# TensorE's program order relisted by due dates, and a rearranged opening with filler products, in a two-layer trunk on eight cores

## Chip, cores, metric

One Trainium2 chip, 8 cores: each computes one sample of the batch. The metric is device time in microseconds, of the slowest core; lower is better. In some executions, whatever the kernel, one die or both run at a lower granted clock (the share of its full clock that TensorE is given) and the time is longer, by up to 18% here. A run is called slow, and left out of times and ratios, when one die's cores took over 1% longer than the other's at a lower clock, or the time is over 1.5% above the kernel's fastest.

## The reference

```python
D_MODEL, BATCH, SEQ, DEPTH, D_FF = 1024, 8, 2048, 2, 2816

def modulate(x, g, mod):                      # mod: shift, scale, gate
    shift, scale, gate = jnp.split(mod, 3, axis=-1)
    h = rmsnorm(x, g) * (1.0 + scale[:, None, :]) + shift[:, None, :]
    return h, gate[:, None, :]

def swiglu(h, w_in, w_out):
    g, u = jnp.split(h @ w_in, 2, axis=-1)
    return (jax.nn.silu(g) * u) @ w_out

def reference(x, c, norm_g, w_mod, b_mod, w_ffn_in, w_ffn_out, ...):
    c_act = jax.nn.silu(c)
    for l in range(DEPTH):
        mod = c_act @ w_mod[l] + b_mod[l]
        mod_f1, mod_mx, mod_f2 = jnp.split(mod, 3, axis=-1)
        h, gate = modulate(x, norm_g[l, 0], mod_f1)
        x = x + 0.5 * gate * swiglu(h, w_ffn_in[l, 0], w_ffn_out[l, 0])
        # ... the mixer (gating and short convolution, or causal pooling) ...
        # ... a second half-step SwiGLU ...
    return rmsnorm(x, final_g)
```

What matters here: no product of layer 0 can start before its shift and scale rows are there (16 rows of the modulation matrix, 512 KB each: 8 MB), and before half of x (two tiles of 2 MB) has been loaded and its statistics taken.

## The kernel before

The program is written as a list of operations, each with what it reads and writes and a modelled cost. A first pass places them in listing order. A second, `relist`, simulates the machine again and lets the engines named in `free` take, of the operations that are ready in the model, the one with the earliest due date; the other engines keep the first pass's order. Each engine then runs its list strictly in order. TensorE was not free: its order was the listing's.

```python
    def relist(self, free=("dve", "act")):
        # ... cost[] and due[] of every operation: due = its start in the first listing
        #     (plus 8 us if it isn't TensorE's), pulled ahead by what depends on it ...
        fixed = {e: [] for e in self.ENGS if e not in free}
        for o in sorted(ops, key=lambda o: (o.start, o.idx)):
            if o.eng in fixed:
                fixed[o.eng].append(o.idx)
        # ... events in order of model time t; for each idle engine e:
                elif e in ready:                       # a free engine
                    if not ready[e]:
                        continue
                    _, x = heapq.heappop(ready[e])     # ready, earliest due
                else:                                  # a fixed engine waits for its next one
                    if at[e] >= len(fixed[e]) or not isready[fixed[e][at[e]]]:
                        continue
```

The opening, where the 16 rows become shift and scale of the 8 chunks of 128 channels: a row's dot product with the conditioning vector is either 8 one-column TensorE matmuls in f32 (16 instructions in the profile) or one VectorE pass. A weight slot is a buffer for one weight piece; its "gate" is the chunk after whose row the slot's load is asked for.

```python
    order0 = [0, 4, 1, 5, 2, 6, 3, 7]                     # order in which chunks are made
    on_pe = (0, 2, 4, 6, 8, 10, 12, 14, 15)               # rows (by position) dotted on TensorE
    rows0 = [q for c in order0 for q in (c, 8 + c)]
    # ... row0_dma(n): one 512 KB load;  row0(k): both rows of chunk order0[k] ...
    for k in range(early // 2):
        row0(k)
    stats0(0)                                             # squares of x, summed by a product of ones
    # ...
    for k in range(ready0, NC):
        row0(k)
        # ... apply_chunk: normalise, scale, shift -> H; h_sums: sums of chunks for the fast product ...
    for s, k in zip(range(NSLOT), (3, 5, 6, 7, 7, 7)):    # "gates" of the six weight slots:
        load_next(s, [("MOD", 0, order0[k])])             # slot s is asked for after chunk order0[k]'s row
    # ...
                if k == 0 and g == 0:
                    run_segs(segs[:X_AT])                 # X_AT = 60
                    late_x()                              # second half of x: two loads of 2 MB
                    bg_add(stats_gen([2, 3]))
                    run_segs(segs[X_AT:-3])
    # ...
    Sd.relist()
```

Of the kernel before, what the change touches and what calls it, by code (L numbers as in the profile page):

```python
# [15 lines left out]
NC = 8  # L16
# [4 lines left out]
EPS = 1e-6  # L21
NSLOT = 6
STAGE = True
X_AT = 60


def keeps(sub, g, part, n):
# [434 lines left out]
def I(name, *a, **k):  # L462
    return lambda E: getattr(E, name)(*a, **k)  # L463
# [4 lines left out]
def build_nc():  # L468
# [28 lines left out]
    NSQ = 4  # L497
    SQ = sb("SQ", [128, NSQ, TT], BF16)
    CB = sb("CB", [128, D], F32)
    CT = sb("CT", [128, 8], F32)  # L500
# [5 lines left out]
    ONES = sb("ONES", [128, 128], BF16)  # L506
# [10 lines left out]
    PS = [nc.alloc_psum_tensor("ps%d" % b, [128, TT], F32) for b in range(8)]  # L517

    Sd = Sched()
# [12 lines left out]
    def c_pe(n):  # L532
        return n / 2400.0 + 0.0026

    def mm(out, lhsT, rhs, start, stop, reads, writes, n=TT):
        return add("pe", I("matmul", out, lhsT, rhs, start=start, stop=stop, skip_group_check=True), reads=reads, writes=writes,
                   cost=c_pe(n))
# [4 lines left out]
    def act(out, in_, func, reads, writes, n=TT, src="ps", **kw):  # L542
        op = add("act", I("activation", out=out, in_=in_, func=func, **kw), reads=reads, writes=writes, cost=c_act(n, src))
        if func in (AF.Silu, AF.Gelu_apprx_tanh):
            op.gate = set(last_root[0])
            table_ops.add(op.idx)
        return op

    def tt_(out, in0, in1, op, reads, writes, n=TT, half=False):
        return add("dve", I("tensor_tensor", out=out, in0=in0, in1=in1, op=op), reads=reads, writes=writes, cost=c_dve(n, half))  # L550

    def stt(out, in0, scalar, in1, op0, op1, reads, writes, n=TT, **kw):
        return add("dve", I("scalar_tensor_tensor", out=out, in0=in0, scalar=scalar, in1=in1, op0=op0, op1=op1, **kw),
                   reads=reads, writes=writes, cost=0.05 + c_dve(n))
# [30 lines left out]
    def Xv(c, t):  # L585
        return X[:, t, c, :]

    def Xk(c, t):
        return ("X", c, t)
# [225 lines left out]
    def bg_add(g):  # L815
        bg.append(g)
        if len(bg) == 1:
            bg_state[0] = 0.0
# [73 lines left out]
    def ones_mm(z, t, of=NC // 2):  # L892
        st = stat_state.setdefault(t, {"n": 0, "b": 6 + t % 2, "of": of})
        b = st["b"]
        mm(PS[b][:], ONES[:], SQ[:, z, :], st["n"] == 0, st["n"] == of - 1, [("SQ", z), "ONES"], [("ps", b)])
        st["n"] += 1
# [34 lines left out]
    def apply_chunk(l, s, p, c, tt, place, dest=None):  # L931
        t = 2 * p + tt
        o = (l * 3 + s) * 8
        sh = l * 72 + s * 24
        tm = tmp_rot.next()
        tt_(TP[:, tm, 0:TT], Xv(c, t), RS[:, t % 2, :], ALU.mult, [Xk(c, t), ("RS", t % 2)], [("TP", tm)])
        ap, key = dest if dest is not None else (place.ap(c, tt), place.key(c, tt))
        act(ap, TP[:, tm, 0:TT], AF.Identity, [("TP", tm)] + fin["k", l, s, c], [key], src="sb",
            scale=AS[:, o + c:o + c + 1], bias=MODT[:, sh + c:sh + c + 1])

    def h_sums(c0, w=2):

        def v(q):
            return H[:, (q * 4 + c0) * TT:(q * 4 + c0 + w) * TT]

        def k(q):
            return [("H", q * 4 + c0 + i) for i in range(w)]

        tt_(v(4), v(1), v(0), ALU.subtract, k(1) + k(0), k(4), n=w * TT, half=True)
        tt_(v(1), v(3), v(1), ALU.subtract, k(3) + k(1), k(1), n=w * TT, half=True)  # L950
        tt_(v(5), v(3), v(4), ALU.subtract, k(3) + k(4), k(5), n=w * TT, half=True)
        tt_(v(6), v(2), v(5), ALU.subtract, k(2) + k(5), k(6), n=w * TT, half=True)
# [547 lines left out]
    add("dve", I("memset", SQ[:, 0, :], 0.0), writes=[("SQ", 0)], cost=0.3)  # L1500
    for b in ALLB:
        mm(PS[b][:], ONES[:], SQ[:, 0, :], True, True, [("SQ", 0), "ONES"], [("ps", b)])
    order0 = [0, 4, 1, 5, 2, 6, 3, 7]
    on_pe = (0, 2, 4, 6, 8, 10, 12, 14, 15)
    early = 6
    mid = 1
    rows0 = [q for c in order0 for q in (c, 8 + c)]
# [4 lines left out]
    def row0_dma(n):  # L1512
        kind, w = places[n % npl]
        if kind == "W":
            ap, keys, dk = WM[:, w, :], [("WM", w)], ("WM", w)
        else:
            ap, keys, dk = Af32[:, w * 1024:(w + 1) * 1024], [("A", 4 * w + x) for x in range(4)], ("AM", w)
        src = wmod0_d[rows0[n]] if n in on_pe else wmod_d[rows0[n]]
        add("sp", I("dma_start", out=ap, in_=src), writes=keys, cost=0.06, dma=dk, nbytes=128 * 4096)
        stage0[n] = (ap, keys)  # L1520
# [3 lines left out]
    def row0(k):  # L1524

        c = order0[k]
        for n, q in ((2 * k, c), (2 * k + 1, 8 + c)):
            ap, keys = stage0[n]
            M = MODT[:, q:q + 1]
            shift = n % 2 == 0  # L1530
            fk = ("MOD", 0, c) if shift else ("ASc", c)
            if n in on_pe:
                b = banks0.next()
                for kc in range(NC):
                    add("pe", I("matmul", PS[b][:, 0:1], ap[:, kc * 128:(kc + 1) * 128], CT[:, kc:kc + 1], start=kc == 0,
                                stop=kc == NC - 1, skip_group_check=True), reads=keys + ["CT"], writes=[("ps", b)], cost=0.43)
                src, sk = PS[b][:, 0:1], [("ps", b)]
            else:
                stt(ap, ap, 1.0, CB[:], ALU.mult, ALU.mult, keys + ["CB"], [("MOD", 0, q)], n=1024, accum_out=M)
                for kk in keys:  # L1540
                    Sd.readers.setdefault(kk, []).append(len(Sd.ops) - 1)
                src, sk = M, [("MOD", 0, q)]
            if n + npl < 16:
                row0_dma(n + npl)
            if shift:
                tt_(M, src, SM[:, SM_BMOD + c:SM_BMOD + c + 1], ALU.add, sk + ["SM"], [fk], n=1)
            else:
                stt(AS[:, c:c + 1], src, SB1[:, c:c + 1], SM[:, SM_G + c:SM_G + c + 1], ALU.add, ALU.mult,
                    sk + ["SB1", "SM"], [fk], n=1)
        fin["k", 0, 0, c] = [("ASc", c), ("MOD", 0, c)]  # L1550
# [3 lines left out]
    for t in range(2):  # L1554
        add("sp", I("dma_start", out=X[:, t, :, :], in_=xT[t].rearrange("p (c k) -> p c k", k=TT)),
            writes=[Xk(c, t) for c in range(NC)], cost=0.06, dma=("X", t), nbytes=128 * 16384)
    for n in range(early, npl):
        row0_dma(n)
    def stats0(t):
        for c in range(NC):  # L1560
            z = sq_rot.next()
            act(SQ[:, z, :], Xv(c, t), AF.Square, [Xk(c, t)], [("SQ", z)], src="sb")
            ones_mm(z, t, NC)
        rstd([t], True, load=(1.3, 0.0) if t == 0 else (0.0, 0.0))

    for k in range(early // 2):
        row0(k)
    stats0(0)
    if mid:
        row0(early // 2)  # L1570
    stats0(1)
    tmp_rot.items = list(range(NTP))
    ready0 = early // 2 + mid
    for k in range(ready0):
        apply_chunk(0, 0, 0, order0[k], 0, HH)
    for k in range(ready0, NC):
        row0(k)
        if k == ready0:
            for j in range(ready0):
                apply_chunk(0, 0, 0, order0[j], 1, HH)  # L1580
                if j % 2 == 1:
                    h_sums(j // 2, 1)
        apply_chunk(0, 0, 0, order0[k], 0, HH)
        apply_chunk(0, 0, 0, order0[k], 1, HH)
        if k % 2 == 1:
            h_sums(k // 2, 1)
    tmp_rot.items = [6, 7]
    for q in range(16):
        done_rows.add(q)
    for b in (0, 1):  # L1590
        mm(PS[b][:], ONES[:], SQ[:, 0, :], True, True, [("SQ", 0), "ONES"], [("ps", b)])
    fin["n", 0, 0] = True
    for s, k in zip(range(NSLOT), (3, 5, 6, 7, 7, 7)):
        load_next(s, [("MOD", 0, order0[k])])
    for lm in range(2):
        for sm in range(3):
# [16 lines left out]
    def late_x():  # L1613
        for t in range(2, 4):
            add("sp", I("dma_start", out=X[:, t, :, :], in_=xT[t].rearrange("p (c k) -> p c k", k=TT)), reads=[("A", ablk(6, 0))],
                writes=[Xk(c, t) for c in range(NC)], cost=0.06, dma=("X", t), nbytes=128 * 16384)

    def run_segs(segs, side=iter(())):

        for n, f in enumerate(segs):  # L1620
            f()
            next(side, None)
            if n == 1:
                while carry:
                    carry.pop(0)()
            pump()
# [12 lines left out]
    for k, ph in enumerate(PHASES):  # L1639
# [4 lines left out]
        if sub[0] == "F":  # L1644
            l, i = sub[1], sub[2]
            s = 2 * i
            for g in range(len(GROUPS)):
# [15 lines left out]
                if k == 0 and g == 0:  # L1663
                    run_segs(segs[:X_AT])
                    late_x()
                    bg_add(stats_gen([2, 3]))
                    run_segs(segs[X_AT:-3])
                else:
# [14 lines left out]
                if pm is not None:  # L1683
                    if pm == 0:
                        add("dve", I("memset", STAT[:, 0, 15:16], 0.0), reads=[("MOD", 0, q) for q in range(144)],
                            writes=["PMFREE", "CB"] + [("WM", x) for x in range(NWM)] + [("ST", x) for x in range(4)], cost=0.05)
# [34 lines left out]
        marks.append((sub, p, t_begin, Sd.tl["pe"].tail()))  # L1721

    add("sp", None, reads=[("OUT", t, c) for t in range(4) for c in (1, 3, 5, 7)], cost=0.01)
    Sd.relist()
    with nc.Block() as block:
        Sd.emit(nc, block)
    nc._sched = Sd
# [33 lines left out]
```

## Time and profile before

| | kernel before |
|---|---|
| time, median of 3 fast runs | 1972.81 us (1972.31 to 1972.99) |
| spans of cores 0 and 1 | 1938.9, 1943.3 us |
| spans of cores 2 to 7 | 1961.1 to 1967.0 us |
| TensorE busy, slowest core | 1920.7 us, 98% of the span |
| first real product (all cores) | 58.2 to 60.1 us |
| TensorE idle from 100 to 165 us | 4.1 to 9.4 us |
| TensorE idle after 165 us | 10.5 to 13.1 us |

The clock row of the page gives the granted clock of TensorE in tenths, in 40 slices of 49 us (9 is 90% or more):

```profile
PEclk9887899999999999999999999999999999999998
```

Slices 2 to 5 (49 to 246 us) are the only dip before the last slice: there lies the throttled stretch that the prediction begins with. "Trip" stands below for such a stretch at a clock of 0.81.

### The profile page before, as it was taken

How to read it: one execution, taken by the hardware profiler on the slowest of the kernel's cores; microseconds unless marked ns; L12 is line 12 of the kernel's file. 1: busy time of each engine (PE TensorE's matmuls, PEld its weight loads, DVE VectorE, ACT ScalarE, POOL GpSimd, SP SyncE). 2: the span in 40 equal slices, each digit the busy share in tenths (PEclk: the TensorE clock that was granted, in tenths of full speed). 3: DMA queues.
4: the chain of work that ended last, by engine and by line, in shares of the span. 5: the costliest groups of instructions: out<-in, count | busy, mean ns of one | idle time of the engine just before them, and what ended most of it. 6: DMA issues, size and time to landing. Idle time of an engine off the chain costs nothing.

```text
span 1967.0 us, 25441 instructions; the slowest of 8 cores (1938.9 to 1967.0 us)
## 1 busy us (share of the span) xinstructions
PE 1920.7 (98%) x8750; PEld 874.8 (44%) x8750; DVE 1695.3 (86%) x3246; ACT 1032.8 (53%) x1738; POOL 172.2 (9%) x330
## 2 busy tenths in 40 slices
PE   6999999999999999999999999999999999999997
PEld 4533444444444444444444444444444444444443
DVE  3867899999798999999988888898998889888865
ACT  4443555455564655465455545564456555574343
POOL 0000000000202000000000000000000000000000
PEclk9887899999999999999999999999999999999998
DMA  9875668786777777776755554555454444445752
GB/s 283 164 186 121 135 130 171 172 171 138 158 161 173 162 152 172 157 154 135 169 105 86 86 86 85 87 97 86 76 86 70 84 84 86 75 75 86 173 87 95
DMA packets 66653, 248.72 MB, mean 126 GB/s; under 512 B 7520, under 2 KB 7648, under 8 KB 66016
## 3 DMA queue, kind: packets, MB, share of 16 engines
q0 software_dynamic: 42192, 153.64, 47.5%
q1 hardware_dynamic: 24336, 93.45, 14.4%
q8 instruction: 74, 1.21, 0.2%
q14 instruction: 51, 0.42, 0.1%
HBM read 392.29 MB, written 8.39 MB: 204 GB/s over the span
## 4 chain that ended last, share of the span: by engine, by line
PE 91%; DMA 4%; DVE 3%; ACT 1%; SPq 0%; issue 0%; DVEq 0%; POOLq 0%
PE ps L463 91%; DMA ACTB<-wmod 2%; DMA SLOTS<-wout 2%; DVE ACTB L463 1%; DVE SLOTS L463 1%; DVE X L463 0%; DVE WMOD L463 0%; SPq L463 0%; ACT PMH L463 0%; DVE TP L463 0%; ACT ps L463 0%; DVE ps L463 0%; ACT TP L463 0%; ACT L463 0%; ACT ACTB L463 0%
## 5 line engine op out<-in xcount | busy, mean ns | idle before, releaser
L463 PE MATMUL ps<-H,SLOTS 128*128 128x512 f16 x5440 | 1215.7, 383 | 6.6 <-ACT ps L463 2.2
L463 PEld LDWEIGHTS ps<-H,SLOTS 128*128 128x128 f16 x5440 | 534.9, 99 | 668.8 <-issue 83.7
L463 ACT ACTIVATE ps<-ps 128x512 f32<-128x512 f32 x684 | 398.0, 582 | 584.8 <-PE ps L463 548.6
L463 PE MATMUL ps<-ACTB,SLOTS 128*128 128x512 f16 x2780 | 622.5, 383 | 1.4 <-DVE TP L463 0.8
L463 PEld LDWEIGHTS ps<-ACTB,SLOTS 128*128 128x128 f16 x2780 | 273.7, 99 | 337.5 <-issue 30.6
L463 DVE TENSOR_TENSOR SLOTS<-SLOTS 128x512 f16<-128x512 f16 x996 | 395.2, 418 | 17.1 <-DMA SLOTS<-wout 8.0
L463 DVE SCALAR_TENSOR_TENSOR X<-ps,GH,X 128x512 f32<-128x512 f32 x424 | 308.3, 746 | 44.6 <-PE ps L463 37.6
L463 ACT ACTIVATE TP<-ps 128x512 f32<-128x512 f32 x400 | 238.0, 595 | 130.8 <-PE ps L463 130.5
L463 DVE TENSOR_TENSOR ACTB<-TP,ps 128x512 f16<-128x512 f32 x368 | 249.3, 684 | 46.4 <-PE ps L463 27.8
L463 ACT ACTIVATE SQ<-X 128x512 bf16<-128x512 f32 x224 | 131.4, 621 | 113.1 <-DVE X L463 57.9
L463 POOL DMA_DIRECT2D SLOTS<-win x176 | 93.1, 530 | 1046.0 <-PE ps L463 974.0
L463 DVE TENSOR_TENSOR TP<-ps,TP 128x512 f32<-128x512 f32 x176 | 121.2, 688 | 65.2 <-ACT ps L463 63.4
L463 DVE SCALAR_TENSOR_TENSOR WMOD<-WMOD,CB 128x1024 f32<-128x1024 f32 x129 | 156.8, 1218 | 2.8 <-DMA WMOD<-wmod 2.6
L463 DVE TENSOR_TENSOR TP<-X,RS 128x512 f32<-128x512 f32 x192 | 129.7, 686 | 12.5 <-ACT ACTB L463 8.5
L463 DVE TENSOR_TENSOR ps<-ps,TP 128x512 f32<-128x512 f32 x176 | 122.4, 696 | 15.2 <-PE ps L463 14.0
L463 DVE TENSOR_TENSOR ACTB<-ACTB 128x1024 f16<-128x1024 f16 (+1 forms) x188 | 104.6, 566 | 1.5
L463 POOL DMA_DIRECT2D SLOTS<-wout x88 | 46.5, 528 | 521.4 <-PE ps L463 521.4
L463 ACT ACTIVATE H<-TP,MODT,AS 128x512 f16<-128x512 f32 x81 | 62.7, 805 | 20.0 <-DVE TP L463 11.9
L463 PE MATMUL ps<-SQ,ONES 128*128 128x512 bf16 x130 | 44.7, 432 | 15.0 <-DVE SQ L463 6.7
L463 ACT ACTIVATE PMH<-TP,MODT,AS 128x512 f16<-128x512 f32 x60 | 47.6, 806 | 18.1 <-DVE TP L463 18.1
L463 ACT ACTIVATE ACTB<-TP,MODT,AS 128x512 f16<-128x512 f32 x51 | 40.8, 806 | 15.4 <-PE ps L463 12.5
L463 DVE TENSOR_TENSOR SQ<-SQ 128x1024 bf16<-128x1024 bf16 (+1 forms) x56 | 36.3, 649 | 12.2 <-ACT SQ L463 11.8
(74 smaller groups left out, 562.0 us busy)
## 6 DMA issues: line engine op xcount, KB each, us to landing
SLOTS<-win POOLq DMA_DIRECT2D x176, 512.0 KB, 6.0
WMOD<-wmod SPq DMA_DIRECT2D x131, 512.0 KB, 5.8
SLOTS<-wout POOLq DMA_DIRECT2D x88, 512.0 KB, 5.4
SLOTS<-wab POOLq DMA_DIRECT2D x28, 512.0 KB, 8.7
X<-xT SPq DMA_DIRECT2D x4, 2048.0 KB, 20.8
outT<-X SPq DMA_DIRECT2D x16, 512.0 KB, 3.7
ACTB<-wmod SPq DMA_DIRECT2D x13, 512.0 KB, 25.1
CB<-cb SPq DMA_DIRECT2D x1, 512.0 KB, 5.5
```

The source lines that it names most:

```text
L463: return lambda E: getattr(E, name)(*a, **k)
```

## The change

Intent: let TensorE step around products whose data is late (the second listing now orders TensorE too); start real products sooner (natural chunk order, so that the first group of chunks is complete early; only four rows dotted on TensorE; the first weight slots asked for sooner); and keep TensorE warm, that is at full clock, until then with 36 filler products of data that is already there. The late half of x, with its statistics, is also asked for five segments earlier in the listing (`X_AT`).

```diff
-X_AT = 60
+X_AT = 55
+WARM = 36
+SLG = (2, 3, 4, 6, 7, 7)
 ...
-    order0 = [0, 4, 1, 5, 2, 6, 3, 7]
-    on_pe = (0, 2, 4, 6, 8, 10, 12, 14, 15)
+    order0 = list(range(NC))
+    on_pe = (10, 12, 14, 15)
 ...                                   (modelled cost of a dot's matmul)
-                                ... writes=[("ps", b)], cost=0.43)
+                                ... writes=[("ps", b)], cost=0.25)
 ...
     stats0(1)
+    for n in range(WARM):
+        op = mm(PS[5][:], ONES[:], SQ[:, n % NSQ, :], True, True, [("SQ", n % NSQ), "ONES"], [("ps", 5)])
+        op.after = 28.0 + n * 0.6
+        op.start, op.end = op.after, op.after + op.issue
 ...
                 apply_chunk(0, 0, 0, order0[j], 1, HH)
-                if j % 2 == 1:
-                    h_sums(j // 2, 1)
 ...
-        if k % 2 == 1:
-            h_sums(k // 2, 1)
+        h_sums(k - 4, 1)
 ...
-    for s, k in zip(range(NSLOT), (3, 5, 6, 7, 7, 7)):
+    for s, k in zip(range(NSLOT), SLG):
 ...
-    Sd.relist()
+    Sd.relist(("dve", "act", "pe"))
```

More of the change, by code (lines that the diff above doesn't have):

```diff
@@ L1535, in row0 @@
                     add("pe", I("matmul", PS[b][:, 0:1], ap[:, kc * 128:(kc + 1) * 128], CT[:, kc:kc + 1], start=kc == 0,
-                                stop=kc == NC - 1, skip_group_check=True), reads=keys + ["CT"], writes=[("ps", b)], cost=0.43)
+                                stop=kc == NC - 1, skip_group_check=True), reads=keys + ["CT"], writes=[("ps", b)], cost=0.25)
                 src, sk = PS[b][:, 0:1], [("ps", b)]
```

## The prediction

> **What bounds the kernel now.** I read the page, then the cores, TensorE by stretch on a slow and a fast core, the first 75 us instruction by instruction, and what TensorE waits for.
>
> ```profile
> span 1967.0 us, 25441 instructions; the slowest of 8 cores (1938.9 to 1967.0 us)
> PE 1920.7 (98%) x8750; PEld 874.8 (44%) x8750; DVE 1695.3 (86%) x3246; ACT 1032.8 (53%) x1738; POOL 172.2 (9%) x330
> ```
>
> TensorE is full. Of the 46 us in which it is not, most lie in the opening. Its count of products is fixed by the algorithm, so time can come only from idle stretches, from products that run at a low clock, and from the opening. The stretches of the slowest core (3), then of core 0, with the granted clock third from the end:
>
> ```profile
> core 3: us, PE busy (x) PEld busy (x) DVE busy (x) ACT busy (x) POOL busy (x), PEclk, DMA share, GB/s
> 50.00:60.00 10.00, 9.60 (x45) 8.99 (x45) 9.21 (x26) 4.70 (x7) 2.12 (x4) 1.00 0.96 177
> ...
> 60.00:230.00 170.00, 163.61 (x619) 66.99 (x618) 129.46 (x249) 77.02 (x128) 11.09 (x21) 0.81 0.69 152
> ```
> ```profile
> 60.00:230.00 170.00, 162.27 (x732) 71.90 (x732) 149.38 (x295) 88.93 (x148) 13.26 (x25) 0.97 0.79 175
> ```
>
> Between 60 and 230 us core 3 gets through 619 products at a clock of 0.81, core 0 through 732 at 0.97. At full clock a product is 0.208 us (48 in 10 us on core 0), so the 113 missing ones are 24 us of the 28 us by which their spans differ. Cores 2 to 7 all have this: 0.81 from some 69 to 229 us, some 160 us, then full clock to the end. Cores 0 and 1 never have it. Busy time hides it.
>
> The opening is a chain of loads of modulation rows (8 MB in 16 rows) and of x, at the full rate of the DMA engines, and then of TensorE's dot products with the last rows:
>
> ```profile
> 48.38 3.55 PE L463 MATMUL ps<-CT,ACTB 128*128 128x1 f32 x16 [2.10 <-DMA ACTB<-wmod]
> 51.79 3.55 PE L463 MATMUL ps<-CT,WMOD 128*128 128x1 f32 x16
> 55.20 3.55 PE L463 MATMUL ps<-CT,ACTB 128*128 128x1 f32 x16
> 59.16 1.01 PE L463 MATMUL ps<-SQ,ONES 128*128 128x512 bf16 x2 [0.40 <-DVE AS L463]
> 59.96 10.46 PE L463 MATMUL ps<-H,SLOTS 128*128 128x512 f16 x42
> ```
> ```profile
> 59.54 0.15 PEld L463 LDWEIGHTS ps<-H,SLOTS 128*128 128x128 f16 x1 [0.28 <-issue]
> 59.96 0.15 PEld L463 LDWEIGHTS ps<-H,SLOTS 128*128 128x128 f16 x1 [0.28 <-issue]
> 60.39 0.15 PEld L463 LDWEIGHTS ps<-H,SLOTS 128*128 128x128 f16 x1 [0.28 <-issue]
> ```
>
> The first real product starts at 59.5 us, and weight loads 0.42 us apart show that TensorE is at half clock then, whatever the "1.00" of the stretch says (core 3's clock record begins only at 61.8 us). The waits after 100 us:
>
> ```profile
> PE ps L463 <- DVE SQ L463: 6.7, 4, 2.5
> PE ps L463 <- DVE CB L463: 3.3, 3, 1.8
> PE ps L463 <- DVE TP L463: 2.7, 2, 1.9
> PE ps L463 <- ACT ps L463: 2.2, 5, 0.7
> ```
>
> Gaps over 0.3 us after 100 us sum to 17.0: 6.3 in 129 to 153 us (late x tiles, second-half statistics), where the clock also falls to 0.5 for 6.8 us, and 10.8 in some fifteen places up to 1956.
>
> [...] a weight piece of 512 KB (1 MB in HBM) issued beside the row loads took 11 us (37.1 to 48.2), alone some 6.
>
> **The change, part by part.**
>
> *Fewer row dots on TensorE (9 to 4).* Five rows go to VectorE at 1.23 + 0.08 = 1.31 us each. Three of these land before 18 us, when VectorE is idle: free. Two come after 33 us: 2.6 us on top of the 23.3 us that VectorE is busy in 30 to 60 us. It fits, narrowly. TensorE is rid of 5 x 3.5 = 17.7 us, mostly spent waiting for loads anyhow.
>
> *Natural order.* A unit's first and fifth products (8 matmuls) need only chunks 0 to 3. Before, chunk 3 came seventh of eight; now it comes fourth, its rows landing near 36 us. So the two groups of units 0 and 1 (16 matmuls; the six PSUM banks let in no more) can run before chunk 7 is done.
>
> *Earlier weight slots.* Slot 0 is asked for at about 18 us rather than 37, slots 1 and 2 at 37 and 41 rather than 49 and 53. No byte is saved; they push back the rows. By the last row's landing (52.2) 1.5 MB of slots had moved; now some 2.7 MB, so at 0.33 MB/us that row lands 3.6 us later, near 55.8.
>
> *Fillers.* 36 products of ones with resident squares, from the end of the squares (near 36 us) on: 36 x 0.43 = 15 us cold, 8 warm, in time that is free. They warm the clock, so that the last dot takes some 2 us (the diff's new cost is 8 x 0.25) rather than 3.5.
>
> Sum of the opening. Before, the first product that needs chunk 7 came after 8 others: 59.96 + 8 x 0.43 = 63.4. Now: last row 55.8, dot 2.0, scale 0.3, normalised chunk 0.7 + 0.8 = 59.6, and 0.6 for VectorE's fuller queue, 60.2. That is 3.2 earlier, with 8 more products done (1.7): **5 us, between 0 and 9.**
>
> *TensorE relisted.* The second listing takes TensorE's operations as they get ready in its model, by due date. Products that wait in the model step aside; waits that the model does not foresee stay. From 129 to 153 us, 6.3 idle and 6.8 x (0.81 - 0.5) = 2.1 of clock: VectorE stood 5.05 us for an output weight piece slowed by the x tiles, which no TensorE order speeds up. I take 2.5 of 8.4. Of the 10.8 later on, a third: 3.5. An order fit to a model makes new waits: minus 2. **Net 4 us.**
>
> *The late x statistics* begin five segments earlier in the listing; the transfer still waits for the same activation block. Counted with the above.
>
> *The limiter.* If it trips on the dense f16 stream as now, its window moves with that stream and nothing changes. If the fillers trip it (25%), the window opens near 45 instead of 69 us and 24 x 0.19 = 4.5 us are saved; if a gentler start leaves every pair of cores untripped (7%), some 28. Expected: 3; I count 2 beside the median.
>
> 5 + 4 + 2 = 11 us off 1972.8: **1962 us.**
>
> **Rivals.** (a) *The opening is DMA-bound and nothing shows.* For: the engines are full (share 0.96 to 1.03) from 10 to 70 us, and earlier slots delay the last rows. Against: the 10 us of dots after 48.4 are TensorE's own, and 16 products need no late row. Time: 1968. (b) *The new order harms.* VectorE is up to 98% busy in a stretch (49.0 of 50 at 820 to 870 us); products taken early fill banks that VectorE must empty, and the model knows neither the 0.81 clock nor real landings. For: waits of TensorE are now small and can only be matched in a well-tuned order. Against: due dates are the first listing's own starts, so it departs from that only where it would stall. Time: 1978. (c) *The limiter goes or its window is spent on fillers.* For: cores 0 and 1 show that the same program can escape. Against: [...] the dense stream that follows is the same. Time: 1938 if all cores escape; a single throttled core keeps the old time.
>
> **Range and chances.** 2% is 39 us. Opening and order together cannot give that; it takes escape from the limiter on every core as well: 5%. To lose 39 us the new order would have to stall TensorE at a hundred places: 2%. Range 1947 to 1973: below, an early trip with a good opening; above, rival b.
>
> **What would show it.** In the profile after: weight loads of the first real products about 0.22 us apart; the first of them before 55 us, with a gap or fillers before the second group; the last rows' landing at 54 to 57 us; the moment when 0.81 begins (69 for "moves with the stream", 45 for "fillers trip it") and its length (160); waits for SQ, CB and TP shorter than 6.7, 3.3 and 2.7; TensorE's gaps after 160 us near 8. I am wrong if the chunk-7 product still starts at 63 us, if the sum of waits after 100 us grows, or if the limiter's length changes.

What was not read from the traces is cut out, and the cuts are marked; no term of the sum went with them, it is still 5 + 4 + 2 = 11 us. "The limiter" is only a name for whatever sets the stretch at 0.81; no trace shows what trips it, so the chances of 25% and 7% behind the 2 us are guesses. The order's 4 us suppose that a late product holds up those behind it, as the pairs of squares did for 1.80 and 2.53 us before 149.7 and 152.9 us (core 3, listed below). The 0.33 MB/us is the rate of core 3 from 10 to 40 us (315 to 333 GB/s). "Slowed by the x tiles" is read from this: the output weight piece was issued at 114.55 us, the two late tiles of x (2 MB each) from 114.81 on, and the piece took 14.22 us where the median of its kind is 5.4.

## The result, and the profile after

The changed kernel takes 1966.09 us, the median of four fast runs (1965.01, 1966.25, 1965.92, 1969.49). Against the kernel before in the same rounds it is 0.9969 (0.995 to 0.9989): 6.7 us less, inside the predicted range and 4 us above the number. Ratios throughout are the mean time of one kernel's fast runs over that of the other's fast runs of the same rounds, so they are not quite the ratio of the medians quoted. The agreement hides a sum whose three terms were all off, two of them in sign.

The page's head and clock row, kernel after:

```profile
span 1963.5 us, 25398 instructions; the slowest of 8 cores (1931.2 to 1963.5 us)
PE 1909.8 (97%) x8706; PEld 861.4 (44%) x8706; DVE 1697.0 (86%) x3256; ACT 1031.9 (53%) x1738; POOL 172.4 (9%) x330
PEclk6898889999999999999999999999999999999999
```

TensorE is busy 10.9 us less (1909.8 for 1920.7). The clock's dip is still there, now in slices 4 to 6. The 6 in slice 1 is no new low: core 3's clock record before begins only at 61.8 us, and other cores of that run, such as core 1 from 9 to 30 us, show the same half clock in the opening. The cores, kernel after:

```profile
core 0: 1960.5 us, clock 0.969
core 1: 1961.7 us, clock 0.970
...
core 3: 1931.2 us, clock 0.986
...
core 6: 1961.4 us, clock 0.968
core 7: 1963.5 us, clock 0.970
```

Two pairs (0-1, 6-7) are throttled, two (2-3, and 4-5 with 1935.7 and 1933.5) are spared, and the spared cores are some 7 us faster than the spared ones of before (1938.9 and 1943.3 against 1931.2 to 1935.7). The slowest core decides, and it is a throttled one. By stretch, throttled core 7 and then spared core 3, kernel after (columns as in the prediction: engines, then granted clock, DMA share, GB/s):

```profile
46.00:67.00 21.00, 17.52 (x71) 13.65 (x72) 12.44 (x32) 9.16 (x13) 1.58 (x3) 0.51 0.90 203
...
123.00:131.00 8.00, 4.28 (x15) 1.38 (x14) 4.91 (x12) 1.18 (x2) 0.53 (x1) 0.83 1.00 276
137.00:297.00 160.00, 159.78 (x611) 65.94 (x610) 131.12 (x248) 76.85 (x130) 10.56 (x20) 0.81 0.58 124
```
```profile
137.00:297.00 160.00, 159.44 (x736) 71.55 (x735) 155.10 (x306) 92.65 (x160) 13.73 (x26) 1.00 0.73 154
```

The 0.81 now opens at 137 us, not 69, on the cores that have it, and again lasts 160 us. Core 7 gets 611 products through, core 3 736. The 125 missing ones at some 0.216 us each (159.44 / 736) are 27 us of the 32 us between their spans. From 46 to 67 us the clock is 0.51 in spite of the fillers, and from 123 to 131 TensorE is idle for 3.7 us. The same stretches, kernel before, throttled core 3 and then spared core 0:

```profile
69.00:229.00 160.00, 153.61 (x578) 62.72 (x577) 120.94 (x231) 70.78 (x118) 11.09 (x21) 0.80 0.67 152
```
```profile
69.00:229.00 160.00, 152.27 (x692) 67.68 (x692) 142.27 (x279) 82.26 (x138) 13.26 (x25) 0.98 0.77 174
```

Even the spared core of before was idle 160 - 152.27 = 7.7 us in that stretch, mostly for the late half's statistics (5.3 us for SQ). A throttled TensorE reaches such waits later and loses less in them (6.4 us in all on core 3). In the new place of the dip, a spared core has 0.6 us of idle time, so that there is next to no waiting in which the slower clock would cost nothing: the missing products alone are 27 us. So the moved dip is a dearer one: 29 us a pair in place of 22 (timed runs, table below). The missing products explain only part of that, 27 us against some 25 before (114 at 0.22 us); the rest of the difference was not traced.

**The opening** is later, not sooner. TensorE of core 7 in order, kernel after (a line is a run of equal instructions; in brackets the idle time before it and what ended it):

```profile
34.66 7.92 PE L465 MATMUL ps<-SQ,ONES 128*128 128x512 bf16 x24 [5.31 <-ACT SQ L465]
...
49.48 0.98 PE L465 MATMUL ps<-CT,ACTB 128*128 128x1 f32 x4 [4.33 <-DMA ACTB<-wmod]
50.32 0.59 PE L465 MATMUL ps<-SQ,ONES 128*128 128x512 bf16 x1
...
61.45 2.13 PE L465 MATMUL ps<-CT,ACTB 128*128 128x1 f32 x10
...
63.82 1.91 PE L465 MATMUL ps<-H,SLOTS 128*128 128x512 f16 x4
```

The 8 products of the statistics and the first 16 fillers run through by 42.6 us, and the record has full clock from 39.5 to 46.4 us (over the cores from 38.6-40.2 to 45.4-47.0); the other fillers are threaded between the dots' matmuls. The first of the four dots is done by 45.1 us. Then TensorE waits 4.33 us for the next row, the clock halves (from 46.4 to 66.8 us in the record), and the other three dots run at half clock with a filler of 0.59 us after every second or fourth matmul. The first real product (63.82) comes after the last dot: the order that the model chose puts all four dots first, and TensorE, which keeps that order, did not start the early products, whose data was there by some 46 us, while a row was late. In the listing, when the kernel is built anew and its modelled times are printed, the last row lands at 44.9 us and slot 0 at 48.2, so the dots rightly go first. On the chip slot 0 landed at 32.2 to 33.4 us and the last row at 55.1 to 56.4. The chain of waits says the same, kernel after, then before (start, length, what):

```profile
12.07 37.27 DMA ACTB<-wmod
49.48 61.13 PE ps L465 x272
111.14 14.93 DMA SLOTS<-wout
...
```
```profile
18.77 29.48 DMA ACTB<-wmod
48.38 6.97 PE ps L463 x32
57.81 1.01 DVE SLOTS L463 x3
...
```

Both chains go through a row load that ends at 48 to 49 us; after it, 6.97 us of dots and a last stretch of VectorE's work stand before the first product of before, 14 us of dots and fillers before the first of after (63.82 - 49.48). Over the cores the first real product moves from 58.2-60.1 to 62.9-64.7 us, and the 200th, on cores unthrottled then, from 103.4-105.1 to 108.2-110.4: the opening loses 5 us.

**The order** gives much more than predicted. What TensorE waits for after 100 us, core 7, kernel after:

```profile
PE ps L465 <- DVE TP L465: 3.7, 1, 3.7
PE ps L465 <- ACT ps L465: 3.3, 6, 0.8
PE ps L465 <- DVE SQ L465: 2.1, 2, 1.8
...
PE ps L465 <- DVE CB L465: 0.3, 1, 0.3
```

SQ went from 6.7 to 2.1 and CB from 3.3 to 0.3; TP and ps (from ACT) rose by 1 each. On all cores, TensorE's idle time from 100 to 165 us fell from 4.1-9.4 to 2.3-4.3 us, after 165 us from 10.5-13.1 to 6.5-8.8. The half clock in that place lasted 6.8 to 10.2 us on every core before, and 3.4 us or none here; in a second profile of the changed kernel (e12) it lasted 6.8 us on four cores and did not come on the others. What has changed in the order is seen where the late statistics are taken, kernel before (core 3), then with the new order alone (run `e1_relist_only` below, core 0):

```profile
147.20 0.70 PE L463 MATMUL ps<-SQ,ONES 128*128 128x512 bf16 x2
149.69 0.68 PE L463 MATMUL ps<-SQ,ONES 128*128 128x512 bf16 x2 [1.80 <-DVE SQ L463]
152.91 1.01 PE L463 MATMUL ps<-SQ,ONES 128*128 128x512 bf16 x2 [2.53 <-DVE SQ L463]
```
```profile
137.38 0.70 PE L463 MATMUL ps<-SQ,ONES 128*128 128x512 bf16 x2
137.91 2.27 PE L463 MATMUL ps<-ACTB,SLOTS 128*128 128x512 f16 x8
...
140.79 0.70 PE L463 MATMUL ps<-SQ,ONES 128*128 128x512 bf16 x2
```

Before, TensorE stood and waited for each pair of squares; now other products go in between. The wait for VectorE (TP) behind a weight piece, somewhat earlier in the program, stays (1.94 us before on core 3, 3.92 us on core 0 of e1).

### The profile page after: what moved, and what is told of

Read it like the earlier page. It is cut to its first block, busy times and chain, and to the rows that moved or that the text cites. A ratio compares the mean times of both kernels' runs of the same rounds, so it can differ in the third digit from the quotient of the medians.

```text
span 1963.5 us, 25398 instructions; the slowest of 8 cores (1931.2 to 1963.5 us)
## 1 busy us (share of the span) xinstructions
PE 1909.8 (97%) x8706; PEld 861.4 (44%) x8706; DVE 1697.0 (86%) x3256; ACT 1031.9 (53%) x1738; POOL 172.4 (9%) x330
## 4 chain that ended last, share of the span: by engine, by line
PE 91%; DMA 4%; DVE 3%; ACT 1%; SPq 1%; issue 0%; DVEq 0%; POOLq 0%
PE ps L465 91%; DMA ACTB<-wmod 2%; DMA SLOTS<-wout 1%; DVE X L465 1%; SPq L465 1%; DMA SLOTS<-win 1%; DVE WMOD L465 0%; DVE ACTB L465 0%; DVE TP L465 0%; DVE SLOTS L465 0%; ACT PMH L465 0%; ACT ps L465 0%; DVE ps L465 0%; ACT L465 0%; ACT TP L465 0%
## 5 line engine op out<-in xcount | busy, mean ns | idle before, releaser
L465 PE MATMUL ps<-SQ,ONES 128*128 128x512 bf16 x166 | 58.9, 438 | 28.9 <-ACT SQ L465 24.9
L465 ACT ACTIVATE H<-TP,MODT,AS 128x512 f16<-128x512 f32 x81 | 62.9, 807 | 20.7 <-DVE TP L465 13.8
```

The lines of the kernel that those rows point to most:

```text
L465: return lambda E: getattr(E, name)(*a, **k)
```

## Experiments

How to read them. Each run on the chip leaves the span of all eight cores. But for the dies that the slow state holds, they fall into two heaps some 20 to 30 us apart, and both cores of a pair (0-1, 2-3, 4-5, 6-7) are always in the same one; where there is a profile, the later heap has the stretch at 0.81 and the earlier has none. So each timed run tells four times whether a pair tripped, and gives the span of spared and of tripped cores apart. Pairs on a die that the slow state holds are left out; a run called slow only because all its trips fell on one die is counted in this table (so e1's 9 of 24 are six runs). Two runs called slow (1984.09 of before on chip 3, 1980.69 of e11), whose slower die has cores up to 18 and 26 us over the tripped ones' median, are counted with that die tripped; without it the counts are 17 of 34 and 11 of 20, and nothing below changes.

| kernel | chip | spared cores, median span | tripped cores | pairs tripped |
|---|---|---|---|---|
| before | 3 | 1942.5 | 1965.0 | 19 of 36 |
| before | 13 | 1942.7 | 1964.8 | 30 of 40 |
| before | 1 | 1943.1 | 1964.0 | 37 of 42 |
| after | first comparison | 1933.5 | 1962.8 | 6 of 16 |
| after (`e12_after_again`) | 1 | 1932.8 | 1961.0 | 15 of 20 |
| `e1_relist_only` | 3 | 1928.0 | 1954.0 | 9 of 24 |
| `e2_open_only` | 3 | 1944.7 | none | 0 of 18 |
| `e3_no_fillers` | 3 | 1932.2 | 1962.0 | 5 of 18 |
| `e4_old_gates` | 3 | 1926.7 | 1952.9 | 2 of 24 |
| `e11_old_gates_again` | 1 | 1927.8 | 1953.0 | 13 of 22 |
| `e5_nofill_oldgates` | 13 | 1927.0 | 1956.1 | 11 of 22 |
| `e6_spread_x` | 13 | 1927.5 | 1953.4 | 10 of 20 |
| `e8_stall` | 13 | 1931.2 | 1956.2 | 4 of 22 |
| `e9_before_pauses` | 1 | 1945.4 | 1971.8 | 12 of 14 |
| `e10_nofill_stall` | 1 | 1929.6 | 1959.4 | 11 of 20 |

The spared column repeats within some 1 us between chips (before: 1942.5, 1942.7, 1943.1; after: 1933.5, 1932.8; old gates: 1926.7, 1927.8) and is the clean measure of the program. The last column is partly the chip's: before trips in 53%, 75% and 88% of its pairs. The medians of before's fast runs are 1971.18 on chip 3, 1971.13 on chip 13 and 1967.09 on chip 1; times below are medians of fast runs.

### The order alone, and the opening alone

`e1_relist_only`, from the kernel before:

```diff
-    Sd.relist()
+    Sd.relist(("dve", "act", "pe"))
```

> The kernel before with TensorE added to the second listing and nothing else of the change. Theory A (the new order gives all the gain, the new opening loses some 5 us): about 1961 us, 12 under before; the product number 8 of the H stream at 62 us on the clock of its core as before; TensorE idle after 165 us about 7 us per core instead of 12, idle from 100 to 165 us about 3 instead of 6. Rival B (the natural order and early slots carry the gain, the order alone does nothing): 1972 us, gaps as before.

Measured: 1958.85 us, 0.9865 (0.9746 to 0.9985), by the 2% rule unclear; the interval is wide because one of three fast runs, 1931.52, had no trip. Spared cores 1928.0: the order is worth 1942.5 - 1928.0 = 14.5 us, more than any other part and more than the whole change gives on the spared cores (1942.5 - 1933.5 = 9.0). So the opening must cost. By the profiles' spared cores (0 and 1 of before, 4 to 7 of e1) the gain is made up of about 2 us before the 200th product, 5 us of idle time from 100 to 165 us, 2.5 us lost to half clock there and 3 us of idle time after it. The waits of TensorE after 100 us, spared core 5:

```profile
PE ps L463 <- ACT ps L463: 3.3, 6, 0.8
...
PE ps L463 <- DVE SQ L463: 1.8, 1, 1.8
```

SQ has shrunk here as in the changed kernel, so that is the order's doing. Idle time from 100 to 165 us is 2.6 to 4.6, after it 6.5 to 9.5.

`e2_open_only`, from the changed kernel. The fillers had to go with the order: with them and TensorE fixed, the second listing deadlocks in its own model and nothing is built.

```diff
-WARM = 36
+WARM = 0
-    Sd.relist(("dve", "act", "pe"))
+    Sd.relist()
```

> The changed kernel without TensorE in the second listing and without fillers: natural chunk order, four row dots on TensorE, early slot gates, statistics at 55. Theory A: the rows land some 4 us later, so the 8th product comes at 64 to 67 us and the time is 1973 to 1978, no better than before. Rival B: 1966 us or less. Gaps after 165 us stay at 12 us.

Measured: 1949.87 us, 0.9887 (0.987 to 0.9904). The time misses the expectation by 20 us and more, because no pair tripped in any fast run, 0 of 18, on a chip where before trips in 19 of 36. The span of spared cores, 1944.7 against 1942.5, is as the theory had it: the opening without fillers loses 2 us in the old order, and its idle times after 100 us are those of before (7 to 8.7, 10.5 to 15.5). The eighth real product (numbered from 0, as in the expectations) came at 64.3 to 65.9 us, 61.4 to 63.5 in the kernel before.

### Which part of the opening costs

`e3_no_fillers` and `e4_old_gates`, each from the changed kernel:

```diff
-WARM = 36
+WARM = 0
```
```diff
-SLG = (2, 3, 4, 6, 7, 7)
+SLG = (3, 5, 6, 7, 7, 7)
```

> The changed kernel with no fillers. Theory A1 (fillers stand between the row dots on TensorE and lengthen them, at half clock, by some 5 us): 8th product at 62 to 63 us instead of 67, time 1961. Rival A2 (it is the rows' late landing, from the early slot gates, that delays): 8th product still at 66 us or later, time 1966. If the first dense stretch now trips the limiter again, 0.81 begins near 70 us instead of 137 and the time stays as these say.

> The changed kernel with the old slot gates (3, 5, 6, 7, 7, 7), fillers kept. Theory A2: the last row lands near 53 us instead of 57 and the 8th product comes at 63, time 1962. Theory A1: rows land earlier but the fillers still stretch the dots; 8th product at 65 or later, time 1965 or more.

Measured: without fillers 0.9893 (0.9794 to 0.9993), unclear, two fast runs with a trip (1964.08, 1965.11) and two without (1937.43, 1936.55); with the old gates 1929.92 us, 0.9815 (0.9747 to 0.9883), unclear as well. By spared spans the fillers cost 1933.5 - 1932.2 = 1.3 us, the earlier gates 1933.5 - 1926.7 = 6.8 us. With the old gates the opening of TensorE, core 0, is:

```profile
44.15 0.58 PE L465 MATMUL ps<-CT,ACTB 128*128 128x1 f32 x4 [3.48 <-DMA ACTB<-wmod]
...
55.67 2.13 PE L465 MATMUL ps<-CT,ACTB 128*128 128x1 f32 x10
...
58.05 1.91 PE L465 MATMUL ps<-H,SLOTS 128*128 128x512 f16 x4
```

The same program with the first weight pieces asked for later: the dot that TensorE waits for starts at 44.2 to 45.0 us over the cores, for 47.8 to 50.3 in the changed kernel, and the first product at 58.0 to 59.3, for 62.9 to 64.7, with all the fillers in place: 5 us sooner. Without the fillers but with the new gates the same dot still waits until 49.08 us (core 3), and the eighth product comes at 64.1 to 65.4 us, against 66.7 to 68.5 with them: the fillers do delay the first products by some 3 us, of which 1.3 are left at the end, little more than the column repeats to. Both of e3's expectations named a time that it missed, A1 (62 to 63) and A2 (66 or later). The rival that blames them is out as the main cause.

Much of the gain in time of this kernel is luck, though: its profile has no trip on any core and only 2 of 24 pairs tripped. Whether the old gates do that, or this chip, needed a repeat elsewhere (below).

`b0_before`, the kernel before itself, one look on the chip of the next three:

> The kernel before once more, for a second profile. If the place where the limiter trips belongs to the kernel, 0.81 begins at some 69 us, 6 to 8 us after the first return to full clock, on the pairs of cores whose span is near 1965; if it is chance, it begins after a later dip of the clock (130 to 150 us) on some pairs.

Measured: 1970.42 us; trips at 69.4 to 69.9 us in three pairs, at 133 us in the fourth.

`e5_nofill_oldgates`, both edits of e3 and e4:

> The changed kernel with the old slot gates and no fillers: natural order, four dots, TensorE relisted. Theory: fillers cost 1 to 2 us in the opening and nothing else, so the spans of cores that the limiter spares are 1924 to 1927 (with fillers: 1926). Rival: the fillers keep the opening gentle or the clock warm, so without them the 8th product comes later than 62.7 us or trips become common (over a quarter of the pairs).

Measured: 1959.24 us, 0.9944 (0.9927 to 0.9962); spared 1927.0, which is e4's 1926.7 without fillers: they are worth nothing there. It also equals e1's 1928.0, so natural order, four dots on TensorE and the late statistics' earlier place together are worth 1 us at most. Trips in three pairs at 132 to 135 us, none at the first return to full clock. In the timed runs half of the pairs tripped, which the rival had given as its sign (over a quarter), but before trips in 75% on this chip; its other sign, a late eighth product, did not come (58.9 to 61.0 us).

### Does a fall to half clock bring the trip?

In the profiles so far every trip began 4 to 8 us after a core of the pair came back from half clock to full. The kernel before comes back to stay at some 62 us and trips at 69; the changed kernel passes that return (66.8), called the first below, unharmed, waits 2 to 4 us at 123 us (in the end for an output weight piece that is issued at 111.14 us, just before the two 2 MB loads of the late half of x at 111.39, and takes 14.93 us, in the chain above, where the median of its kind is 5.3), falls to half clock, comes back, and trips at 137. Theory: the returns bring the trips, and a return into gapless work does so more easily. (Where the record reaches back so far, the clock is also full for 3 to 10 us at a time between 27 and 50 us; no trip came there.) The next kernels try to take away or add returns and gaps.

`e6_spread_x`, from e4: the late half of x in eight loads of 512 KB, spread over the first units, so that no weight piece is issued beside 4 MB.

```diff
-X_AT = 55
+X_UNITS = (3, 4, 5, 6, 7, 7, 8, 8)
 ...
-    def late_x():
-        for t in range(2, 4):
-            add("sp", I("dma_start", out=X[:, t, :, :], in_=xT[t]...  reads=[("A", ablk(6, 0))], ...
+    def late_x(n, kk):
+        t, c = 2 + n // 4, 2 * (n % 4)
+        add("sp", I("dma_start", out=X[:, t, c:c + 2, :], in_=xT[t][:, c * TT:(c + 2) * TT]...  reads=[("A", ablk(kk, 0))], ...
```

> Old slot gates, fillers, TensorE relisted, and the late x tiles in eight pieces of 512 KB spread over units 3 to 8 instead of two of 2 MB at once. Theory (the limiter trips on dense work after a fall to half clock, and the fall comes from the wait for the weight piece behind the x tiles): no gap over 1 us between 100 and 165 us, no fall of the clock after the opening on any core, no trip in any fast run, span 1922 to 1925 on all cores, time 1926. Rival (trips are chance or come from the opening): trips in some pairs all the same, 0.81 without a fall of the clock before it.

Measured: 1955.16 us, 0.9935 (0.9906 to 0.9964), 10 of 20 pairs tripped, spared 1927.5. The gap at 136 us stayed on three cores (2.2 to 3.4 us, on two of them with a fall), and in the profile one pair tripped at 69.3 us, at the first return. So removing the later gap is neither done nor enough.

`e8_stall`, from e6: the gap is forced on all cores, by four GpSimd clears of 1.8 us that the products near 128 us must wait for.

```diff
+                    run_segs(segs[at:-7])
+                    for _ in range(NSTALL):
+                        add("pool", I("memset", PMHf[:, 0:2048], 0.0), reads=[("A", ablk(9, 0))],
+                            writes=["STALL"] + [("ST", i) for i in range(4)], cost=2.0)
+                    stall.append("STALL")          # every product of these segments reads it
+                    run_segs(segs[-7:-3])
```

> The same as the one with spread x tiles, but with TensorE made to wait some 4 us near 125 us by four memsets on GpSimd. Theory: every core falls to half clock there; dense work follows, and in a good part of the pairs (over a quarter) 0.81 begins 4 to 9 us after the clock is back, for 160 us: time about 1955 to 1960 where a pair trips, 1930 where none does. Rival (a stall costs only its own length): 4 to 6 us more than the spread version on all cores and no trips.

Measured: 1946.88 us, 0.9881 (0.9823 to 0.994; two fast runs near 1935, two near 1958.6). Seven of eight cores did fall to half clock at 130 to 133.5 us; no pair tripped in the profile, 4 of 22 in the timed runs. The expectation failed: a return is not enough. After this one TensorE still had gaps of 1.2 to 2.2 us on six cores, but on cores 0 and 1 none over 0.7 us, and that pair did not trip either.

`e9_before_pauses`, the kernel before with two pauses of TensorE soon after its first return, made in the same way after the 16th and the 28th product (from `PAUSE_AFTER = (3, 6)`; each a clear of 1024 columns that waits for one segment and holds up the next).

> The kernel before with two pauses of TensorE of some 1.2 us each (a memset on GpSimd between two groups of products) after its 16th and 28th product, that is some 2 and 5 us after the clock is back at full. Theory (the limiter trips when the first 8 us after the return to full clock are dense): no 0.81 at 69 us on any core, where the two profiles of the kernel before have it on 6 of 8 pairs; trips may come later, at 130 to 145 us, after the second fall of the clock. Rival (the trip has nothing to do with how dense that stretch is): 0.81 at about 69 to 72 us in 2 to 4 pairs again, and 2 us more on every span.

TensorE of core 2, and its later stretch:

```profile
64.50 2.75 PE L464 MATMUL ps<-H,SLOTS 128*128 128x512 f16 x12 [1.16 <-POOL PMH L464]
68.41 7.93 PE L464 MATMUL ps<-H,SLOTS 128*128 128x512 f16 x36 [1.16 <-POOL PMH L464]
```
```profile
80.00:120.00 40.00, 40.00 (x188) 18.08 (x185) 32.18 (x63) 19.83 (x34) 3.17 (x6) 1.00 0.78 180
137.00:297.00 160.00, 154.26 (x579) 63.09 (x578) 128.64 (x243) 73.53 (x122) 10.14 (x20) 0.79 0.54 119
```

Measured: 1977.32 us, 1.0048 (1.0025 to 1.007). With the pauses no core is at 0.81 at 69 us (clock 1.00 from 80 to 120), where before had three of four pairs in each of two profiles. Then the later fall, at 122 to 125 us, takes its turn: trips at 133.5 to 137 us in three pairs, and the kernel is slower than before although its spared cores lose only 2 us. That shows the price of a late trip in an otherwise equal program: 1971.8 - 1945.4 = 26 us, against 21 for the early one of before on this chip (1964.0 - 1943.1).

`e10_nofill_stall`, from e8:

```diff
-WARM = 36
+WARM = 0
```

> Old slot gates, no fillers, spread x tiles, and the stall near 128 us: idle time within 8 us of the return to full clock both in the opening (0.2 to 1.3 us in the kernel with no fillers and old gates) and at the second fall. Theory: trips in fewer than one pair in eight, spared spans 1930 to 1933, median time 1934. Rival (dense or not makes no odds): trips in a third to half of the pairs as in the versions without the stall on the same chip, time 1958.

Measured: 1963.0 us, 0.9976 (0.9957 to 0.9994), 11 of 20 pairs tripped where under one in eight was expected. In the profile none tripped at the first return, two pairs did at 147.7 and 141.6 us: the stall became gaps of 1.5 and then 3 to 5 us, followed by work without gaps. It did not do what it was built for, and the expectation failed.

### The same kernels on another chip

`e11_old_gates_again` is e4 and `e12_after_again` is the changed kernel, unedited, on the chip where before trips most.

> The kernel with the old slot gates and fillers once more, beside the changed kernel on one chip. If that it was nearly free of trips (2 of 24 pairs) belongs to it: at most 4 of some 24 pairs, median 1930 to 1935. If it was the chip: a third or more of the pairs, median 1954 to 1958. Spared spans 1926 to 1928 either way.

> The changed kernel as it is, beside the one with the old gates on the same chip. Spared spans 1933 to 1935, that is 7 us over the old gates; with trips (6 of 16 pairs in its first runs) 1962 to 1966.

Measured: old gates 1956.18 us, 0.994 (0.9922 to 0.9958), 13 of 22 pairs tripped, and trips in the profile at 67.3 to 70.3 us in three pairs, after a first return into work without a gap. So it was the chip, or its luck, that kept e4 free, not the gates; their 5 to 7 us on spared cores stand (1932.8 to 1927.8). The changed kernel: 1966.09 us, 0.9994 (0.9975 to 1.0012), no gain that shows on this chip. Three of its four pairs tripped in the profile, at 136 to 141 us. The throttled stretch of core 2 in e11, and core 4 in e12:

```profile
69.00:229.00 160.00, 159.64 (x608) 66.13 (x609) 128.74 (x252) 73.67 (x124) 11.60 (x22) 0.81 0.69 154
```
```profile
137.00:297.00 160.00, 159.53 (x611) 66.13 (x611) 132.19 (x250) 76.09 (x128) 11.09 (x21) 0.82 0.58 127
```

In both a throttled TensorE is busy all through and gets some 610 products done, whatever the place. The early stretch is cheaper by the table (25 us in e11, 28 in e12). The likely reason is that part of it would be waiting without a trip: from 100 to 165 us the two spared cores of e11 are idle for 1.9 and 3.1 us, the tripped ones for 0.4 at most.

Over the 14 profiles, 26 of 27 trips began 4.1 to 7.8 us after a return from half clock on a core of the pair; the 27th (e12, 136.3 us) came some 9 us after gaps of 2.6 and 1.7 us that brought no fall. At the first return, of 20 pairs with at least 0.3 us of idle time on a core in the next 7 us none tripped; of 36 pairs without, 10 did, and none of the changed kernel's 8 among them. The kernels of the two groups ran on different chips in part, and none of the five kernels with idle time has fillers, so this suggests a rule and doesn't prove one; e9 is the one direct test, with one profile. Nor does every return bring a trip: of 40 pairs, untripped till then, on which a core came back between 110 and 160 us, 16 tripped and 24 didn't.

## Why the predicted time was right and its terms were not, point by point

*What bounds the kernel: right.* TensorE is full (98% of the span busy), so idle time, clock and opening are what is left. The three terms of the sum, predicted -5, -4, -2:

*Opening, -5 us, range 0 to 9: wrong in sign, +5.5* (spared cores, after 1933.5 against e1 1928.0). Its own sub-steps: that the last row "lands 3.6 us later, near 55.8" gave the right time (55.1 to 56.4 us) by luck. The 52.2 that it starts from is the landing of the 17th load of the modulation matrix, which no dot of the opening reads; the 16th, the last row, landed at 50.9 on that core (49.9 to 51.8 over the cores), so the rows came some 5 us later, not 3.6. Three steps on it failed. That "the two groups of units 0 and 1" "can run before chunk 7 is done": on core 7 the first four products could by their data (slot 0 at 33.4 us, their parts of H by some 46), but they stand after the dots in TensorE's list, since the model has the last row before slot 0 (44.9 and 48.2 us) and the chip had it after (55.6 and 33.4). "They warm the clock, so that the last dot takes some 2 us": after the first fillers the clock was full, from 39.5 us, but it halved at 46.4, in a 4.3 us wait, and stayed so to 66.8 us, and the last dot, spread out by fillers, took from 59.7 to 63.6. And the base: the shift of rows was booked for the last row only, but it holds up the earlier ones as well (the one TensorE waits for, 44.2 to 45.0 with the old gates of e4, 47.8 to 50.3 here), and the dots follow each other from there.

So by the prediction's own signs the opening was wrong: the first product did not come "before 55 us", its weight loads were 0.43 us apart and not 0.22, and the first one that needs chunk 7 ran at some 67 us (core 7), not at 60.2; "still starts at 63 us" was to be a sign of being wrong. The gates are 5 to 7 of these us by e4 and e11; the fillers about 1 by e3, nothing by e5; the rest of the opening next to nothing. Rival (a) named the cost, a row delayed by earlier slots, and was nearer than the main line.

*Order, net -4 us: right in sign, too small: -14.5* by e1. The step that failed is the 2.5 of 8.4 us in 129 to 153 us, taken on the ground that "no TensorE order speeds up" VectorE's wait for a weight piece. On core 3 only 1.94 of those 6.3 us of idle time hang on that piece, and that wait did stay (TP). The other 4.3 are the late statistics' products (SQ), which the new order steps around: SQ 6.7 to 2.1, and by e1 5 us of idle time and 2.5 us lost to half clock less. The 2 us that the order wins before the 200th product were not booked at all. And the minus 2 for new waits: TP and ps rose by 2.1 together. Idle time of 3.5 us after 165 us to be won was about right (10.5-13.1 to 6.5-8.8, some 4).

*Limiter, -2 us beside the median: the window did not open where it was forecast.* In the prediction the window "moves with that stream and nothing changes", or the fillers open it near 45 us. It moved to 137 us, with the dense stream on from 67, after a later fall to half clock. There it covers work without waits, and costs 29 us in place of 22. Which pairs pay is chance: 6 of 16 and 15 of 20 in two sessions. Since one tripped pair of four sets the time, the 9 us won on the spared cores reach the time as 2 to 3 (tripped cores, median: 1965.0 on chip 3, 1964.0 on chip 1; after 1962.8 and 1961.0). The first comparison's 6.7 us and e12's nothing lie on either side of that figure; what separates them is not settled beyond chips and runs.

So: +5.5 - 14.5 + 7 = -2 for the time of a run with a trip, -9 for one without; predicted -11, measured -6.7 once, -1.0 the second time (1966.09 - 1967.09). The number was near by cancelling errors. Rival (b), that the new order harms, is out by e1, and rival (c) by the runs: every fast run of the changed kernel had a trip, and none opened at 45 us. What would have been better is seen in the runs: the order with the old gates, e4 and e11, is ahead of the kernel before on two chips, at 0.9815 (unclear, mostly the luck of few trips) and 0.994 (its interval, 0.9922 to 0.9958, lies below 1), and the changed one where both ran (1956.18 against 1966.09 on chip 1). The order alone, e1, has the same spared span as it, so the gain is the order's.

Open: why a return trips one pair and not another; why chips differ; whether gaps after a return protect, or only did so by chance; the part of X_AT alone, which no run isolates (with the natural order and dots it is at most 1 us).

## What to carry to other kernels

Where the clock adds a price to some cores and not to others (20 to 30 us here), read spared and throttled cores apart: the time of the slowest core alone would have put the old gates at 36 us by one comparison (1966.09 - 1929.92) and 10 by another (1966.09 - 1956.18), where they are worth 5 to 7. Where loads bound the opening (DMA share 0.96 to 1.03 from 10 to 70 us, kernel before), a later buffer asked for earlier held up what was in front of it: with the new gates the dot that waits for its row started at 47.8 to 50.3 us instead of 44.2 to 45.0, and the first product 5 us later. A list fixed by a model's landing times (last row 44.9 us, slot 0 48.2; on the chip 55.6 and 33.4) turned the delay into an in-order wait; check the landing of the first operand that each engine stands for, not only the last. Letting the bounding engine be ordered by readiness too was the best single edit here by the spared cores (14.5 us), and it cost one word.

## What the traces show of the clock

- The stretch at 0.81 takes pairs of cores (0-1, 2-3, 4-5, 6-7), lasts 158 to 163 us and lifts under the same load: core 7 of the changed kernel has it from 137.7 to 296.3 us, 157.78 us busy from 138 to 296, and stands at 1.00 from 297 to 1954 us, 1647.90 us busy of 1657. Which pair is taken changes from run to run and chip to chip: 19 of 36, 30 of 40 and 37 of 42 pairs for one and the same kernel.
- 26 of 27 trips came 4.1 to 7.8 us after a return from half to full clock, at 69 us or, in the changed kernel, not until 137 us of a load that is dense from 67 us on.
- In the changed kernel, gaps of 2.62 and 2.08 us that ended at 126.0 and 125.4 us (cores 0 and 6) went with a fall to half clock, from 125.4 and 125.3 us for 3.4 us; gaps of 2.04 and 2.34 us (cores 3 and 5, each followed by one of 0.52 us) did not. Such a fall preceded a trip that cost 29 us. That the fall brought the trip is suggested by these runs and not proven.
- Not all work brought full clock: from 46.4 to 66.8 us TensorE ran one-column f32 dots with 0.59 us fillers between them, 17.52 us busy in the 21 us from 46 to 67, and stayed at a clock of 0.51. Dots without fillers did no better: core 1 of before, 9.60 us busy from 50 to 60 us, stood at 0.50. On core 3 of before full clock came some 2 us after the first real product (59.96 and 61.82 us), after 10 us of dots that took 0.21 us each (0.11 at full clock, core 0 from 38.6 to 41.9 us). What mix of work decides is not shown.
- The clock record begins late on some cores (core 3 of before at 61.8 us), and the windows show 1.00 for what lies before it: so for 50 to 60 us there, where weight loads 0.42 us apart are those of half clock.
